# A decoder step on one core: the paged-cache stream ended earlier, and the second half's output projection moved in between two pairs of the first half's feed-forward slices

## The chip, the cores and the metric

The kernel runs on one core of a Trainium2 chip. Five engines take instructions from queues of their own, each in the order in which the program was built: PE (TensorE, matrix products; its weight loads are listed apart as PEld), DVE (VectorE), ACT (ScalarE), POOL (GpSimd) and SP (SyncE, which here only issues transfers). They wait for one another through semaphores. The metric is the time of one execution in microseconds (us) of device time; lower is better. Products accumulate in PSUM, everything else is held in SBUF, and large arrays lie in the memory outside.

## The reference

One layer of a hybrid decoder, for a prompt of 1024 tokens and for 8 sequences of 8 new tokens each that look back on 8192 cached positions. Cut to what matters:

```python
n = rmsnorm(h, g_mix);  u = n @ w_in                    # 1024 -> 2224 columns
o_gla = gated_linear_attention(u...)                    # 4 heads, chunked
q, ckv, krope = latents(u...)                           # MLA: 8 heads, latent width 128
o_mla = attend(q, ckv, krope)     # prompt: causal over 1024; sample: over 8192 cached positions
h = h + concat(o_gla, o_mla) @ w_o                      # output projection, 1024 x 1024
n = rmsnorm(h, g_ffn)
a, c = n @ ffn_w_gate, n @ ffn_w_up                     # 1024 -> 2816 each
h = h + (silu(causal_conv3(a)) * c) @ ffn_w_down        # 2816 -> 1024
h = h + (p @ ple_w_proj) * sigmoid(rmsnorm(h, g_ple) @ ple_w_gate)

def sample_attention(...):        # for each of 64 pages per sequence
    c, r = pool_ckv[page], pool_krope[page]             # gathered through the page table
    k, v = latent_to_kv(c, r)                           # keys are normalised per head
    stats = combine(stats, block_stats(q, k, v))        # running maximum, sum, weighted values
```

All products are made from float32 numbers that are split in two: a rounded high part and a low part, and three products (high x high, high x low, low x high) stand for one.

## The kernel before

There are two streams of work. The **cache stream** (`cache_stream`) attends the 8 sample sequences to their pages: 64 blocks of 1024 positions each. For a block, two indirect transfers on POOL's queue gather latents (`craw`) and rotary keys; PE transposes them (`ctp`, `crp`) and multiplies them with the key weights and the absorbed queries (`ks`: three products for each of two halves of each of eight row groups, so 48 a block and 3120 in all with the sequences' own new rows). ACT squares the keys (`csq`) and copies the scores (`sn`); DVE sums the squares (`css`); then ACT, DVE and POOL make the scale, the maximum (`mt`, with two small products on PE), the exponentials (`phl`), and PE multiplies with the latents (`cpv`, eight products). After the last block `po_mla` takes the result through the value weights and leaves it in `oTm`, which the output projection of the sample rows reads.

The **dense stream** (`dense`) does everything else, in this order: the input projections of the prompt's first and second half of 512 rows (`prompt_half`), gated linear attention, the prompt's causal attention, the first half's output projection (`wo_half(0)`), and the first half's 22 feed-forward slices of 128 columns (`ffn_half(0)`). Slices go in pairs: `ff_chunk` makes the gate and up products of a slice (`ps_gu`), and `down` multiplies a pair with its rows of the down weights (`ps_dn`) and adds them to the residual `h`. Behind the dense stream and not interleaved with the cache stream come the second half's output projection (`wo_half(1)`, which takes the 64 sample rows with it: `ps_ds`), the second half's feed-forward slices (`ffn_half(1)`), and the gated layer embedding.

How the two streams are mixed is set by a loop that emits a step of the cache stream whenever its due time is not past the work of the dense stream so far; each cache step moves the due time on by 4.4 times an entry of `PACE`, one entry for each part of the dense stream. What the loop emits goes to a scheduler that orders each engine's instructions by its own model of when they can run, with the emitted order as priority; so the order on the engines is fixed when the program is built, and is near the emitted one but not equal to it.

The second half's part needs space that the cache stream holds: three PSUM banks (`psK`) and a region of SBUF (`cp`). Both are given back at `ph1.close()`, after the loop, and then become `psT` (transposes and one more bank) and `xr`, which holds the second half's residual `h1`, the sample rows `hs`, the normalised and transposed input `X1`, and more. `wo_half` ends with the second normalisation: `renormer` takes a row tile's sum of squares on ACT (`junk`), the scale on POOL (`rs`), the scaled rows on DVE or on ACT and POOL (`xs`), transposes on PE in groups of four (`pt`), and a split by ACT and DVE into `X`. `ff_chunk` reads `X` whole.

## Time and profile before

| | |
|---|---|
| time, median of 3 runs | 2305.02 us (2301.93 to 2313.23) |
| the profiled execution: time / span | 2310.78 us / 2309.1 us |
| granted PE clock over the span | 0.985 |
| busy: PE, DVE, ACT, POOL | 2205.9, 1567.9, 1403.6, 1023.9 us |
| first and last score product of the cache stream (`ks`) start at | 68.1 and 1653.6 us |
| `po_mla` runs at | 1675.0 us |
| transfers over the span | mean 90 GB/s |

The span is divided here into the input projections (to about 400 us), gated linear attention (to about 600 us), the prompt's attention (to about 1005 us), the first half's output projection (to about 1100 us), its feed-forward slices with the cache stream beside them (to 1656 us), the end of the cache stream (to 1677 us), the second half's output projection (to 1730 us), its normalisation (to 1756 us), and the second half's feed-forward slices and the layer embedding. A view by windows gives for each stretch how long each engine was busy; PE's busy time subtracted from the length is time in which PE stood still. PE is counted as busy from the first to the modelled end of overlapping products, so two products of 512 columns that each last 0.39 us may start 0.23 us apart. The clock column is the share of full speed that PE was granted.

### The profile page before, as it was taken

How to read it: one execution, taken by the hardware profiler on the slowest of the kernel's cores; microseconds unless marked ns; L12 is line 12 of the kernel's file. 1: busy time of each engine (PE TensorE's matmuls, PEld its weight loads, DVE VectorE, ACT ScalarE, POOL GpSimd, SP SyncE). 2: the span in 40 equal slices, each digit the busy share in tenths (PEclk: the TensorE clock that was granted, in tenths of full speed). 3: DMA queues.
4: the chain of work that ended last, by engine and by line, in shares of the span. 5: the costliest groups of instructions: out<-in, count | busy, mean ns of one | idle time of the engine just before them, and what ended most of it. 6: DMA issues, size and time to landing. Idle time of an engine off the chain costs nothing.

```text
span 2309.1 us, 38976 instructions
## 1 busy us (share of the span) xinstructions
PE 2205.9 (96%) x13855; PEld 1952.7 (85%) x13855; DVE 1567.9 (68%) x2590; ACT 1403.6 (61%) x3758; POOL 1023.9 (44%) x1223
## 2 busy tenths in 40 slices
PE   7999999999999999999999999999798999999999
PEld 6889888788888888878788888878667999999999
DVE  5765684778878788878755666666677656666642
ACT  6666666768788888876655467767635323232431
POOL 6665675766867777664532234444313000000100
PEclk9999999999999999999999999999898999999999
DMA  5343343323322122143332232222142223232131
GB/s 185 110 133 112 102 152 124 100 69 96 95 75 64 58 58 60 40 143 110 90 93 85 85 100 79 78 78 67 39 138 74 85 81 91 75 92 74 52 116 39
DMA packets 228531, 207.67 MB, mean 90 GB/s; under 512 B 41326, under 2 KB 190291, under 8 KB 228339
## 3 DMA queue, kind: packets, MB, share of 16 engines
q1 hardware_dynamic: 216051, 163.23, 23.5%
q0 software_dynamic: 12288, 41.95, 5.8%
q8 instruction: 111, 1.82, 0.3%
q14 instruction: 81, 0.66, 0.1%
HBM read 178.56 MB, written 26.53 MB: 89 GB/s over the span
## 4 chain that ended last, share of the span: by engine, by line
PE 54%; ACT 5%; DVE 5%; DMA 4%; POOL 3%; issue 2%; POOLq 0%; SPq 0%; DVEq 0%; ACTq 0%
PE ps_gu L137 6%; PE ps_gu L138 6%; PE ps_gu L139 6%; PE ps_dn L137 4%; PE ps_dn L138 4%; PE ps_dn L139 4%; PE ks L137 3%; PE ks L139 2%; PE ks L138 2%; PE ps_pg L139 1%; PE ps_pg L137 1%; PE ps_pg L138 1%; PE cpv L605 1%; PE ctp L518 1%; DMA stg<-ffn_w_gate 1%
## 5 line engine op out<-in xcount | busy, mean ns | idle before, releaser
L542 ACT ACTIVATE csq<-ks 128x256 f32<-128x256 f32 x1040 | 389.2, 400 | 91.1 <-PE ks L139 85.1
L547 DVE TENSOR_REDUCE css<-csq 128x16 f32<-128x1024 f32 (+1 forms) x264 | 315.9, 1197 | 81.0 <-ACT csq L542 75.4
L138 PE MATMUL ps_gu<-X,guh 128*128 128x320 f32 (+2 forms) x1056 | 349.0, 331 | 0.0
L139 PE MATMUL ps_gu<-X,gul 128*128 128x320 f32 (+2 forms) x1056 | 348.4, 330 | 0.0
L137 PE MATMUL ps_gu<-X,guh 128*128 128x320 f32 (+2 forms) x1056 | 348.3, 331 | 0.1
L137 PE MATMUL ks<-mv0h,cTh 128*128 128x256 f32 (+1 forms) x780 | 249.2, 320 | 10.6 <-ACT sn L544 7.3
L138 PE MATMUL ks<-mv0l,cTh 128*128 128x256 f32 (+1 forms) x780 | 225.8, 291 | 0.0
L139 PE MATMUL ks<-mv0h,cTl 128*128 128x256 f32 (+1 forms) x780 | 222.4, 292 | 0.0
L139 PEld LDWEIGHTS ps_gu<-X,gul 128*128 128x128 f32 x1056 | 199.9, 189 | 14.4
L138 PEld LDWEIGHTS ps_gu<-X,guh 128*128 128x128 f32 x1056 | 199.7, 189 | 14.6
L137 PEld LDWEIGHTS ps_gu<-X,guh 128*128 128x128 f32 x1056 | 199.3, 189 | 15.0 <-ACT X L116 0.4
L116 ACT CAST guh<-stg 128x512 fp32r<-128x512 f32 x188 | 111.4, 620 | 149.2 <-PE ps_gu L138 70.4
L137 PE MATMUL ps_dn<-wdh,sh 128*128 128x512 f32 x480 | 188.4, 400 | 3.6 <-DVE h L1406 2.6
L138 PE MATMUL ps_dn<-wdl,sh 128*128 128x512 f32 x480 | 189.1, 394 | 0.0
L139 PE MATMUL ps_dn<-wdh,sl 128*128 128x512 f32 x480 | 179.7, 395 | 0.0
L1406 DVE TENSOR_TENSOR h<-h,ps_dn 128x512 f32<-128x512 f32 x240 | 154.4, 680 | 34.3 <-PE ps_dn L139 33.9
L137 PEld LDWEIGHTS ks<-mv0h,cTh 128*128 128x128 f32 x780 | 148.1, 190 | 33.2 <-ACT sn L544 16.6
L574 POOL TENSOR_TENSOR chl<-craw,chl 128x1024 fp32r<-128x1024 f32 x64 | 141.8, 2215 | 62.7 <-ACT chl L573 62.1
L117 DVE TENSOR_TENSOR gul<-stg,guh 128x512 fp32r<-128x512 f32 x138 | 94.5, 708 | 101.3 <-ACT guh L116 97.6
L138 PEld LDWEIGHTS ks<-mv0l,cTh 128*128 128x128 f32 x780 | 148.3, 190 | 7.8 <-issue 1.3
L593 POOL TENSOR_TENSOR phl<-sn,phl 128x512 fp32r<-128x512 f32 (+1 forms) x64 | 85.8, 1340 | 147.5 <-ACT phl L592 147.3
L139 PEld LDWEIGHTS ks<-mv0h,cTl 128*128 128x128 f32 x780 | 145.8, 189 | 1.2
(556 smaller groups left out, 6302.4 us busy)
## 6 DMA issues: line engine op xcount, KB each, us to landing
stg<-ffn_w_gate SPq DMA_DIRECT2D x88, 256.0 KB
stg<-ffn_w_up SPq DMA_DIRECT2D x88, 256.0 KB
stage<-ffn_w_down SPq DMA_DIRECT2D x88, 256.0 KB
stage<-w_in SPq DMA_DIRECT2D x48, 256.0 KB
stage<-w_o SPq DMA_DIRECT2D x32, 256.0 KB
h<-x_prompt SPq DMA_DIRECT2D x8, 512.0 KB
oraw<-doT SPq DMA_DIRECT2D x16, 256.0 KB
stg<-ple_w_gate SPq DMA_DIRECT2D x16, 256.0 KB
```

The lines of the kernel that those rows point to most:

```text
L116: act.copy(hi, src)
L117: (lo_eng or dve).tensor_tensor(lo, src, hi.bitcast(F32), ALU.subtract)
L137: pe.matmul(ps, ah, bh, start=first, stop=False)
L138: pe.matmul(ps, ah, bl, start=False, stop=False)
L139: pe.matmul(ps, al, bh, start=False, stop=last)
L518: pe.transpose(tp[:, i, :], craw[:, i, :], ident)
L542: act.activation(sq[:, f * 256:f * 256 + 256], ks[:, 0:256], AF.Square)
L547: dve.tensor_reduce(o.ss[:, g0 + i + 1 - n:g0 + i + 1, :].rearrange("p i h -> p (i h)"), sq2[:, :n].rearrange("p i (h n) -> p (i h) n", n= ...
L574: pool.tensor_tensor(ch[:, c0:c1, 128:256], src, ch[:, c0:c1, 0:128].bitcast(F32), ALU.subtract)
L593: pool.tensor_tensor(phl[:, :nt, 64:128], sb, phl[:, :nt, 0:64].bitcast(F32), ALU.subtract)
L605: pe.matmul(pv[:, 0:258], phl[:, i, :], o.ch[:, i, :], start=i == 0, stop=i == nt - 1)
L1406: dve.tensor_tensor(h, h, ps, ALU.add)
```

## The change

Four things are changed.

- The nine entries of `PACE` become smaller (the first from 2.0 to 1.41, the last from 1.34 to 1.1), so the loop emits cache steps at shorter intervals of dense work, and the stream is used up within the fourth pair of `ffn_half(0)`, as emitted.
- `dense` runs the first nine pairs of `ffn_half(0)` (slices 0 to 17), then asks for whatever is left of the cache stream (`z["drain"]`), then runs `wo_half(1)`, and then the last two pairs (slices 18 to 21). Their `down` takes its PSUM banks from the wider rotation `both`.
- The exchange of the cache stream's space for `psT` and `xr` becomes a function, `second_pools`, that is called when the cache stream has been emitted whole, in the middle of the first half's slices.
- `wo_half(1)` no longer ends with the last steps of its normalisation: these are called once right after it and after each of the two slices of the last pair. Its row tiles 4 to 7 are scaled in buffers of `xr` (`ptl`, `pth`). The first feed-forward weights of the second half are asked for before the last `down` of the first half.

```diff
-PACE = [2.0, 1.5, 2.2, 1.65, 1.6, 1.0, 1.45, 1.37, 1.34]
+PACE = [1.41, 1.088, 1.601, 1.168, 1.142, 0.708, 1.035, 1.1, 1.1]
+LASTG = 18
...
-        yield from ffn_half(0)
+        yield from ffn_half(0, range(0, LASTG, 2))
+        z["drain"] = True
+        yield 0.0
+        yield from wo_half(1)
+        z["step"](None)
+        for g in range(LASTG, NF, 2):
+            for f in (g, g + 1):
+                yield from ff_chunk(f, 0)
+                if g == NF - 2:
+                    z["step"](None)
+            if g == NF - 2:
+                ff_weights(0, 1)
+            yield from down((g, g + 1), both, 0)
...
-          (False, 4): "cca", (False, 5): "sca", (False, 6): "guh", (False, 7): "gul", (False, 8): "pth",
+          (False, 4): "ptl", (False, 5): "pth", (False, 6): "ptl", (False, 7): "pth", (False, 8): "pth",
...
-            step = renormer(False, p2t if hf else pd) if g == 3 else None
+            step = None
             if g == 3:
-                ff_weights(0, hf)
+                step = z["step"] = renormer(False, p2t if hf else pd)
                 if hf:
                     step(NT)
+                else:
+                    ff_weights(0, hf)
             yield from down(grp, bank, hf, step)
-        step(None)
-        step(None)
+        if not hf:
+            step(None)
+            step(None)
...
+    def second_pools():
+
+        ph1.close()
+        z["psT"] = ctx.enter_context(tc.tile_pool(name="psT", bufs=2, space=PSUM, reuse_waits="tile"))
+        xr = z["xr"] = ctx.enter_context(tc.tile_pool(name="xr", bufs=1, side="right", reuse_waits="tile"))
+        z["h"].append(xr.tile([P, 4, D], F32, name="h1"))
+        z["X"].append(xr.tile([P, 8, 2, 512 + R], F32R, name="X1"))
+        z["hs"] = xr.tile([R, D], F32, name="hs")
+        z["cout"] = xr.tile([P, 18, NF], F32, name="cout")
...
-        if live_c and (not live_d or due <= tdense):
+        if live_c and (not live_d or due <= tdense or "drain" in z):
             due += 4.4 * PACE[z["part"]]
             live_c = next(cs, done) is not done
             ncache += 1
+            if not live_c:
+                second_pools()
...
-    run(wo_half(1))
```

Three places show what the order becomes on the engines. First PE at the end of the cache stream. Before, the last score products stand among the products of the first half's eleventh pair, and these rows follow (`cpv`, `mt`, `pt_ol` and `po_mla` are the cache stream's last steps, `ps_dn` is the eleventh pair's, `ps_ds` the second half's output projection for the sample rows):

```order
L139 MATMUL ps_dn<-wdh,sl 128x512
L605 MATMUL cpv<-chl,phl 128x258 x8
L581 MATMUL mt<-ident,ml 128x128
L588 MATMUL mt<-ident,bm 128x64
L605 MATMUL cpv<-chl,phl 128x258 x8
L627 MATMUL pt_ol<-ident,acclo 128x64
L668 MATMUL po_mla<-oTm,WvT 64x64 x8
L1418 MATMUL ps_ds<-wdh,oTg 128x512
```

Now the last score products stand in the sixth pair, and `po_mla` stands among the gate and up products of the seventh:

```order
L139 MATMUL ps_gu<-X_14671,guh 128x512
L140 MATMUL ps_gu<-X_14671,gul 128x512
L669 MATMUL po_mla<-oTm,WvT 64x64 x8
L138 MATMUL ps_gu<-X_14671,guh 128x512
L139 MATMUL ps_gu<-X_14671,guh 128x512
```

What moved is the place of the stream's last steps: before, no dense product stood between them; now there are 49 products of 512 columns between the last score product's block and the first `mt`, 33 more up to the last `cpv`, and 54 from there to `po_mla`.

Second, PE at the end of the second half's output projection, where the normalised rows `xs` are transposed (`pt`). Before, the last products of the projection are followed by the transposes and then by the first gate products of the second half, whose operand `X` is what the transposes make:

```order
L139 MATMUL ps_dn<-wdh,sl 128x512
L1474 MATMUL pt<-ident,xs 128x64 x8
L1474 MATMUL pt<-ident,xs 128x128 x16
L137 MATMUL ps_gu<-X_21044,guh 128x256 x2
L1474 MATMUL pt<-ident,xs 128x128 x4
L138 MATMUL ps_gu<-X_21044,guh 128x256
```

Now the tenth pair of the first half follows the projection, and the transposes stand among its products (the sample rows' after 34 of them, the first prompt tile's, shown here, after 61):

```order
L138 MATMUL ps_gu<-X_14671,guh 128x512
L1487 MATMUL pt<-ident,xs 128x128 x4
L139 MATMUL ps_gu<-X_14671,guh 128x512
L1487 MATMUL pt<-ident,xs 128x128 x4
L140 MATMUL ps_gu<-X_14671,gul 128x512
```

What moved is the first reader of `X1`: it now comes two pairs after the projection, and what stands between reads the first half's `X`.

Third, ACT in the first half's input projections, where `G` takes four projected gate chunks out of PSUM. Before, these rows stand around the first two of them (`chl`, `cTh`, `kTh` and `csq` are the cache stream's; `w`, `st` and `gsf` the dense stream's):

```order
L161 COPY st<-ps_sm 64x256
L116 CAST w<-stage 128x4x128 x2
L689 COPY G<-ps_pj 128x512
L573 CAST chl<-craw 128x8x128
L689 COPY G<-ps_pj 128x512
L289 COPY gsf<-ps_sm 64x128
```

Now, from the first of them on:

```order
L690 COPY G<-ps_pj 128x512
L507 COPY sr<-csr 128x512
L557 ACTIVATE cy<-css,epst_68 128x64
L599 ACTIVATE mb<-bm 128x1
L558 ACTIVATE cy<-cy 128x64
L559 ACTIVATE ca<-cy 128x64
L543 ACTIVATE csq<-ks 128x256 x2
L545 COPY sn<-ks 128x64
L543 ACTIVATE csq<-ks 128x256
L117 CAST cTh<-ctp 128x512
```

More of the cache stream stands between two dense steps. Counted on PE, the score products that stand ahead of the second half's input projections are 309 before and 384 now; ahead of gated linear attention's first gate product 597 and 771; ahead of the first product of the first half's output projection 2244 and 2496; ahead of its first gate product 2412 and 2700. ACT's loads of a function table, which stand where the functions of the feed-forward slices and of the cache stream alternate, are 63 before and 43 now.

More of the change, by code (lines that the diff above doesn't have):

```diff
@@ L1514, in conv_state, with wo_half @@
         z["prv"] = prev.rearrange("p (b j f) -> p f b j", b=8, j=2)
-    def wo_half(hf):
+    def wo_half(hf, pairs=range(4)):
         bank = z["both"] if hf else pd
-        if hf:
-            sp.dma_start(z["hs"], A["x_sample"].rearrange("b t d -> (b t) d"))
-        for t in range(4 * hf, 4 * hf + 4):
-            sp.dma_start(hrows(t), A["x_prompt"][0, t * P:(t + 1) * P, :])
-        for g in range(4):
+        if pairs[0] == 0:
+            if hf:
+                sp.dma_start(z["hs"], A["x_sample"].rearrange("b t d -> (b t) d"))
+            for t in range(4 * hf, 4 * hf + 4):
+                sp.dma_start(hrows(t), A["x_prompt"][0, t * P:(t + 1) * P, :])
+        for g in pairs:
             grp = (2 * g, 2 * g + 1)
@@ L1612, in ff_chunk, with ffn_half @@
         chunks[f] = (sh, sl, ss_) + wdown(A["ffn_w_down"][0][fs, :])
-    def ffn_half(hf, hooks={}):
+    def ffn_half(hf, groups=range(0, NF, 2), hooks={}):
         bank = z["both"] if hf else pd
-        for g in range(0, NF, 2):
+        for g in groups:
             for f in (g, g + 1):
@@ L1622, in ffn_half, with p2t, p2, both @@
                 down_sample([chunks[c][2:] for c in (g, g + 1)], bank)
+    def p2t(shape, name):
+        return z["psT"].tile(shape, F32, tag="t", name=name)
+    def p2(shape, name):
+        return z["psT"].tile(shape, F32, tag="b", name=name, bufs=1)
+    turn = [0]
+    def both(shape, name):
+        turn[0] = (turn[0] + 1) % 6
+        return (pd, pm, pd, pm, pd, p2)[turn[0]](shape, name)
+    z["both"] = both
+    def second_pools():
[6 more added lines that the diff above has]
+        z["cout"] = xr.tile([P, 18, NF], F32, name="cout")
     dn = dense()
```

20 lines of the change are left out of this document (2 added, 18 removed).

## The prediction

> **What bounds the kernel now.** I read the page first. PE is busy nearly all the time and the other engines are not, so what can be won is time in which PE stands still or runs at a lower clock, and the slices show where that is: the 29th to the 31st, with 7, 9 and 8 in PE's row and 8, 9 and 8 in the clock's.
>
> ```profile
> span 2309.1 us, 38976 instructions
> PE 2205.9 (96%) x13855; PEld 1952.7 (85%) x13855; DVE 1567.9 (68%) x2590; ACT 1403.6 (61%) x3758; POOL 1023.9 (44%) x1223
> PE   7999999999999999999999999999798999999999
> PEclk9999999999999999999999999999898999999999
> ```
>
> Then the view by windows, cut at the stages (columns: length, busy time of PE, PEld, DVE, ACT and POOL, granted clock, transfers):
>
> ```profile
> core 0: us, PE busy (x) PEld busy (x) DVE busy (x) ACT busy (x) POOL busy (x), PEclk, DMA share, GB/s
> 140.00:250.00 110.00, 108.63 (x731) 100.55 (x730) 56.98 (x94) 67.45 (x200) 66.56 (x77) 1.00 0.39 125
> 250.00:400.00 150.00, 141.60 (x869) 125.86 (x868) 99.81 (x175) 99.99 (x293) 96.33 (x103) 0.99 0.41 129
> 600.00:1005.00 405.00, 391.54 (x2676) 341.54 (x2676) 326.40 (x542) 345.99 (x1027) 295.35 (x302) 1.00 0.22 63
> 1100.00:1350.00 250.00, 244.73 (x1195) 203.48 (x1195) 164.48 (x234) 137.23 (x296) 87.34 (x90) 0.99 0.31 92
> 1350.00:1656.00 306.00, 296.43 (x1617) 251.79 (x1617) 212.46 (x303) 224.23 (x534) 122.91 (x110) 0.99 0.24 74
> 1656.00:1677.00 21.00, 6.49 (x37) 5.22 (x35) 4.40 (x12) 5.08 (x10) 5.92 (x5) 0.58 0.16 52
> 1677.00:1730.00 53.00, 49.86 (x205) 37.91 (x205) 41.41 (x66) 20.08 (x39) 5.63 (x6) 0.97 0.39 126
> 1730.00:1756.00 26.00, 14.76 (x88) 12.84 (x88) 19.75 (x25) 19.74 (x51) 15.96 (x23) 0.74 0.17 52
> 1756.00:2200.00 444.00, 443.95 (x2926) 418.22 (x2927) 276.80 (x514) 154.44 (x309) 45.92 (x120) 1.00 0.27 81
> ```
>
> PE's idle time is the length less the busy time: 1.4 and 8.4 us in the two stretches of the input projections, 13.5 us in the attention, 5.3 and 9.6 us in the first half's slices, then 14.5 us of 21 at the cache stream's end and 11.2 us of 26 at the second normalisation. From 1756 us on there is nothing left to win. Two short stretches hold 25.7 us of idle time, and the waits of PE there say on what:
>
> ```profile
> PE mt L581 <- POOL ml L569: 7.9, 1, 7.9
> PE pt L1474 <- DVE X L117: 5.3, 3, 2.3
> PE pt L1474 <- POOL xs L1464: 4.4, 2, 3.8
> PE cpv L605 <- POOL phl L593: 3.5, 1, 3.5
> ```
>
> The first and the fourth are the last block of the cache stream going through ACT, POOL and DVE with no other product in the queue; the other two are the rows of the second half on their way to `X`.
>
> **The change, part by part.** *The cache stream's end.* Its chain, from the last score product (PE's timeline, then the chain of waits):
>
> ```profile
> 1653.19 0.30 PE L139 MATMUL ks<-mv1h,cTl 128*128 128x320 f32 x1
> 1653.33 0.28 PE L137 MATMUL ks<-mv0h,cTh 128*128 128x256 f32 x1
> 1653.45 0.28 PE L138 MATMUL ks<-mv0l,cTh 128*128 128x256 f32 x1
> 1653.57 0.27 PE L139 MATMUL ks<-mv0h,cTl 128*128 128x256 f32 x1
> ...
> 1655.10 0.40 PE L137 MATMUL ps_dn<-wdh,sh 128*128 128x512 f32 x1
> 1655.34 0.39 PE L138 MATMUL ps_dn<-wdl,sh 128*128 128x512 f32 x1
> ```
>
> ```profile
> 1664.80 0.49 PE mt L581
> ...
> 1669.96 2.10 PE cpv L605 x8
> ...
> 1675.03 1.97 PE po_mla L668 x16
> ```
>
> Products of 512 columns start about 0.23 us apart (1655.10 to 1655.34). The last score product starts at 1653.57; `mt` is 11.2 us behind it, `cpv` 16.4, `po_mla` 21.5. In the new order 49, 82 and 136 products of the sixth and seventh pair stand ahead of these three, which is 11.3, 18.9 and 31.3 us of cover. The chain gets ACT, DVE and POOL no longer alone, and `mt` has nothing to spare, so I leave 1 us (bounds 0, where the cover suffices, and the old 14.5): -14.5 + 1.
>
> *The second normalisation.* It now has the tenth and eleventh pair beside it. The old starts of the transposes, on PE's timeline:
>
> ```profile
> 1731.33 0.46 PE L1474 MATMUL pt<-ident,xs 64*128 64x64 f32 x4 [1.39 <-DVE xs L1461]
> ...
> 1736.25 1.11 PE L1474 MATMUL pt<-ident,xs 128*128 128x128 f32 x4 [3.79 <-POOL xs L1464]
> ```
>
> PE had done the projection 1.39 us before 1731.33; the sample rows come at that time and the first prompt tile 6.3 us after it. The new order puts 34 and 61 products ahead of them, 7.8 and 14.0 us. But DVE must now scale two row tiles ahead of the multiplication that frees a PSUM bank of the tenth pair, so some waiting will return: I take 3 us, between 0 and the old 11.2, nearer to the covered end: -11.2 + 3. The projection's own 3.1 us of idle time stay: its weights pass the same three staging buffers. The new buffers for the scaled rows are first used again in the second half's slices, where PE has no idle time; moving the pools issues no instruction. Both at nothing.
>
> *The clock.* In both stretches PE is granted about half speed (length, PE busy, clock, transfers):
>
> ```profile
> 1660.00:1670.00 10.00, 1.20 (x4) 0.50 0.00 0
> 1670.00:1680.00 10.00, 7.37 (x32) 0.51 0.65 233
> 1730.00:1740.00 10.00, 3.15 (x16) 0.72 0.29 84
> 1740.00:1750.00 10.00, 7.48 (x38) 0.60 0.16 52
> ```
>
> Busy time times the missing share is 0.6 + 3.6 + 0.9 + 3.0 = 8.1 us. Where PE has products throughout, the rows around show 1.00, so this goes with the idle time: -8.1.
>
> *The first half's slices.* They hold 708 score products before (3120 less 2412) and 420 now (less 2700), in the same dense manner while they last, about 100 a pair: 9.6 us of idle time (1350 to 1656 us) for about 520 of them (by the order, from the seventh pair on) gives 7.2 for the some 390 that the order has behind the first pair, and the thinner pairs' idle time, 1.2 us behind the start, falls away: -3.6 (bounds 0 and -6). ACT also loses table loads, 63 before and 43 now. One and what follows it, in the chain of waits:
>
> ```profile
> 1654.55 1.28 ACT L556
> 1655.85 0.35 ACT cy L556
> ```
>
> The next function starts 0.02 us after the load, so 20 x 1.28 = 25.6 us of ACT go. I count them at nothing, since PE's idle time there already holds what of them PE felt. [...]
>
> *The denser stages.* 174 more score products (771 less 597), 3.6 blocks of 48, run before linear attention, and 78 more between there and the output projection. The work is moved, not added; only more idle time costs. At 0.12 to 0.14 us from one score product to the next (1653.19 to 1653.45) 174 are 23 us, so 140 to 400 us becomes about 290 us with the stream's other products. There is room in the first part:
>
> ```profile
> 160.00:180.00 20.00, 20.00 (x107) 16.97 (x106) 2.42 (x7) 6.95 (x17) 9.68 (x8) 1.00 0.39 111
> 320.00:340.00 20.00, 18.15 (x132) 17.06 (x131) 18.89 (x32) 13.25 (x44) 15.99 (x17) 1.00 0.49 157
> ```
>
> DVE and ACT are idle most of the first slice; in the second DVE is busy 94% of the time and PE idle 9%. If all became like 250 to 400 us (5.6% idle): 290 x 0.056 = 16.2 against 9.8 now, +6.5. If all became like the slice at 320: 26.8, +17. If PE filled its holes with the moved work: down to -3. The first is the nearest row, the same work a little denser: +6.5. The attention, with ACT busy 85% and PE idle 3.3%, gets its part of the 78, on 1647 before (2244 less 597), so some 5% more of the stream: 0, at worst 5% idle, +7.
>
> *The sum:* -13.5 - 8.2 - 8.1 - 3.6 + 6.5 = -26.9 us on the profiled execution's 2310.8 (its span 2309.1 and 1.7 around it), so 2283.9. The median of the runs is 5.8 lower, 2305.0; the same difference gives 2278.1, and I say 2278.
>
> **The rivals.** *SP held up.* The loads of `hs` and `h1` need the cache stream's space, and SP waits for it with the feed-forward weights behind. Before, that wait was 20.1 us, and the four transfers followed it:
>
> ```profile
> SPq L1520 <- PE cpv L605: 20.1, 1, 20.1
> ...
> 1672.70 2.00 SPq L1522 DMA_DIRECT2D h<-x_prompt  x4
> ```
>
> 2.25 MB at the 233 GB/s of the window at 1670 are 9.7 us more, 30 us in all. Now they stand between the two down loads of the eighth pair's first slice. The weights behind them are first needed after the seventh pair's second slice, its `down` and the eighth's first slice: about 144 products, 33 us. So it decides from 33 us on. As SP comes there when `po_mla` is due a microsecond or two later, I expect about 12 us, hidden; if SP came a full wait early and the loads were slow, up to 20 us would be seen: 2298.
>
> *The denser stages eat the gain.* At the worst rows above, +17 and +7 in place of +6.5, and no gain in the slices: 2278 + 17.5 + 3.6 = 2299. For it: DVE's 94% at 320 us. Against it: the two slower engines are busy 52 to 67% over 140 to 400 us.
>
> *Slower.* Place: the input projections. The 3.6 moved blocks could run there as the last block does at 1656, each with its chain exposed: 14.5 us of idle time a block, 52 us, 2278 - 6.5 + 52 = 2323.5. It outweighs the 33.4 us of the other terms from 64% exposure on. Against it: the present stream runs there at 1.3 to 5.6% of idle time, with dense products between its steps, and only ahead of the queue's end was nothing there to fill.
>
> *PE's busy time hides room.* Weight loads (PEld) cover 81% of 1100 to 1350 us and 94% from 1756 us on:
>
> ```profile
> L138 PEld LDWEIGHTS ps_gu<-X,guh 128*128 128x128 f32 x1056 | 199.7, 189 | 14.6
> ```
>
> If the loads set the pace, the five pairs that now run without the stream (5 x 144 x 0.23 = 166 us) could be up to 13% faster: 21 us, 2257. Against it: a load of 0.19 us in the 0.23 to 0.24 us from one product of 512 columns to the next is 79 to 83% already, so these pairs stand at their pace. [...]
>
> *The change does not do what it says.* In the order the stream ends in the sixth pair, not the fourth, but three pairs still stand between it and the moved projection, and it can't slip further: the order is fixed. It is part of the forecast.
>
> **How the numbers follow.** About 0.5% (11.5 us) is what a measurement of this kernel can tell from no change. Forecast, 2268 to 2293: 0.62. More is won (PE's holes filled, the slices at their best), about 2262: 0.07. Hidden room, 2257: 0.03. SP held up, 2285 to 2298, half of it within 0.5%: 0.08. Denser stages eat the gain, about 2299: 0.12. Slower, about 2324: 0.08. So faster 0.62 + 0.07 + 0.03 + 0.04 = 0.76, same 0.12 + 0.04 = 0.16, slower 0.08. The range 2258 to 2300 leaves out the slower case, half of the denser one and the lowest, some 0.17 in all.
>
> **What would show it.** Right: in the new profile `po_mla` lies far ahead of the second half's `ps_ds` with PE busy around both; the waits of `mt` for `ml` and of `pt` for `xs` are gone or under 2 us each; the clock is 1.00 from the cache stream's end to the layer embedding; idle time up to 400 us grows by less than 10 us. Wrong: idle time before 1000 us that grows by more than 25 us, with `ks` or `crp` waiting for ACT and DVE; a hole in the eighth pair with `guh` or `wdh` late; or a half clock at the two new borders.

## The result, and the profile after

| | before | after |
|---|---|---|
| time, median of 20 runs each | 2308.58 us (2301.93 to 2315.36) | 2313.19 us (2307.01 to 2320.55) |
| ratio after to before, 95% interval | | 1.0018 (1.0009 to 1.0027) |
| span of the profiled execution | 2309.1 us | 2310.9 us |

The change does not pay: 0.2% slower, inside the 0.5% that count as no change. The forecast was 2278 us, and its range ended at 2300. The page of the kernel after (the busy times and the two rows of slices):

```profile
span 2310.9 us, 38951 instructions
PE 2213.8 (96%) x13855; PEld 1952.6 (84%) x13855; DVE 1574.1 (68%) x2590; ACT 1379.8 (60%) x3738; POOL 1027.6 (44%) x1223
PE   7989998999999999999999999899999999999999
PEclk9989999999999999999999999999999999999999
```

The hole of the 29th to 31st slice is gone, and so is its lower clock. In its place there are 8s in PE's third, seventh and 26th slice, the third with a lower clock as well, and PE is busy 7.9 us longer with the same 13855 products.

The new place does what was wanted. From the view by tile of `ps_ds` and from PE's timeline after (the number in brackets is the idle time ahead of the instruction):

```profile
L1431 PE MATMUL ps_ds<-wdh,oTg x8: 389/395/499, 1617.8 to 1637.3; 128*128 128x512 f32 x8
```

```profile
1499.15 0.79 PE L138 MATMUL ps_dn<-wdh,sh 128*128 128x512 f32 x1 [4.10 <-DVE cv L1620]
1502.91 0.27 PE L582 MATMUL mt<-ident,ml 128*128 128x128 f32 x1
1511.16 1.12 PE L606 MATMUL cpv<-chl,phl 128*128 128x258 f32 x8
1525.25 1.15 PE L669 MATMUL po_mla<-oTm,WvT 128*64 128x64 f32 x16
```

`po_mla` (1525.25) stands 92 us ahead of the first sample product (1617.8), and `mt` and `cpv` start without any idle time ahead of them. The view by windows after, from ahead of the stream's end to the second normalisation's end, and the second half's slices:

```profile
1450.00:1500.00 50.00, 43.92 (x222) 36.07 (x221) 33.72 (x44) 33.21 (x69) 19.85 (x17) 0.99 0.20 58
1500.00:1527.00 27.00, 27.00 (x126) 21.31 (x126) 16.70 (x32) 12.18 (x21) 4.88 (x6) 0.95 0.28 81
1700.00:1752.00 52.00, 48.52 (x211) 38.44 (x210) 29.27 (x43) 19.14 (x38) 11.83 (x16) 0.97 0.28 86
1752.00:2177.00 425.00, 425.00 (x2769) 399.17 (x2768) 266.99 (x497) 144.74 (x292) 48.83 (x120) 1.00 0.28 82
```

The stream's end (1500 to 1527) has no idle time at all, where it had 14.5 us; its clock is 0.95, behind the wait of 4.10 us just ahead of it. What was won here, and 1.8 us more by the spans, must have been lost elsewhere. The same view, cut at the same places of the program in both kernels (columns as in the prediction: length, busy time of PE, PEld, DVE, ACT, POOL, granted clock, transfers): the four parts of the input projections, linear attention, and the first half's slices to the second normalisation's end. Before:

```profile
0.00:144.50 144.50, 124.04 (x695) 109.70 (x696) 97.93 (x199) 94.98 (x293) 91.15 (x138) 0.94 0.45 139
144.50:230.20 85.70, 85.15 (x594) 78.53 (x592) 42.44 (x72) 52.03 (x145) 47.68 (x46) 1.00 0.40 130
230.20:328.20 98.00, 92.71 (x529) 81.81 (x530) 70.44 (x139) 68.88 (x225) 69.52 (x92) 1.00 0.38 117
328.20:407.10 78.90, 74.40 (x498) 68.35 (x496) 45.26 (x59) 48.43 (x131) 50.42 (x53) 0.98 0.46 139
407.10:602.80 195.70, 189.66 (x1426) 164.45 (x1427) 151.47 (x256) 148.06 (x488) 142.61 (x199) 1.00 0.31 90
...
1119.40:1744.00 624.60, 587.16 (x2978) 488.52 (x2978) 417.42 (x601) 382.18 (x863) 218.19 (x213) 0.97 0.28 84
```

And after:

```profile
0.00:149.90 149.90, 125.28 (x693) 111.55 (x694) 101.32 (x202) 96.16 (x294) 92.20 (x139) 0.91 0.44 134
149.90:253.40 103.50, 102.25 (x719) 94.53 (x718) 60.99 (x93) 69.88 (x204) 65.80 (x67) 1.00 0.36 115
253.40:375.20 121.80, 111.84 (x656) 100.49 (x654) 93.92 (x168) 87.37 (x290) 82.59 (x98) 0.97 0.35 109
375.20:452.90 77.70, 74.11 (x505) 68.16 (x503) 33.75 (x53) 50.21 (x131) 50.15 (x57) 1.00 0.49 142
452.90:668.20 215.30, 208.37 (x1496) 177.28 (x1497) 161.98 (x274) 158.90 (x514) 145.03 (x202) 0.98 0.29 82
...
1202.80:1751.80 549.00, 527.29 (x2555) 430.40 (x2554) 359.45 (x523) 294.98 (x640) 170.17 (x169) 0.99 0.30 91
```

The stages hold different numbers of score products now, so their lengths can't be compared as they stand. To compare them I give every product its own time: the usual interval from one product of its shape to the next in the profile of before (0.118 us for a score product of 256 columns, 0.146 for one of 320, 0.231 for 512 columns; the value that 40% of the intervals stay under). All products together have 2083.2 us in every kernel of this case. This is an estimate: with the usual interval taken a little differently the losses of single stages shift by up to 6 us, in all kernels alike, and the changes between kernels by less than 1.5 us. What a stage takes beyond its products' own time is its loss, whether PE is seen idle, runs at half clock, or is held up for so short that the records still show it busy. The 225.9 us of loss before and the 227.7 after divide like this (us):

| stage | loss before | after | change | of it idle | at half clock | inside PE's busy time |
|---|---|---|---|---|---|---|
| input projections | 60.6 | 74.6 | +14.0 | +8.6 | +5.2 | +0.1 |
| linear attention | 20.2 | 31.7 | +11.5 | +0.9 | +3.3 | +7.3 |
| attention, first half's output projection | 70.3 | 73.7 | +3.4 | +2.0 | -1.8 | +3.2 |
| first half's slices, second half's output projection and normalisation | 63.5 | 40.6 | -22.9 | -15.7 | -4.9 | -2.2 |
| from there to the end | 11.3 | 7.2 | -4.1 | | | |

27 us are won at the new place, and 29 are lost ahead of it, by the order that was made denser to let the stream end early.

### The profile page after: what moved, and what is told of

It is laid out like the page before. It is cut to its first block, busy times and chain, and to the rows that moved or that the text cites. A ratio compares the mean times of both kernels' runs of the same rounds, so it can differ in the third digit from the quotient of the medians.

```text
span 2310.9 us, 38951 instructions
## 1 busy us (share of the span) xinstructions
PE 2213.8 (96%) x13855; PEld 1952.6 (84%) x13855; DVE 1574.1 (68%) x2590; ACT 1379.8 (60%) x3738; POOL 1027.6 (44%) x1223
## 4 chain that ended last, share of the span: by engine, by line
PE 72%; DVE 10%; ACT 8%; DMA 4%; POOL 3%; issue 3%; SPq 0%; DVEq 0%; ACTq 0%; POOLq 0%
PE ps_gu L138 6%; PE ps_gu L139 6%; PE ps_gu L140 6%; PE ks L138 4%; PE ps_dn L138 4%; PE ks L140 4%; PE ps_dn L139 4%; PE ks L139 4%; PE ps_dn L140 4%; PE cpv L606 2%; PE ctp L519 2%; PE ps_lt L279 2%; DVE css L548 1%; PE ps_pj L138 1%; PE ps_pg L140 1%
## 5 line engine op out<-in xcount | busy, mean ns | idle before, releaser
L1419 DVE TENSOR_TENSOR h<-h,ps_dn 128x512 f32<-128x512 f32 x240 | 154.3, 680 | 40.6 <-PE ps_dn L140 40.2
L118 POOL TENSOR_TENSOR gul<-stg,guh 128x512 fp32r<-128x512 f32 x50 | 68.7, 1394 | 183.7 <-ACT guh L117 183.5
```

The source lines that it names most:

```text
L118: (lo_eng or dve).tensor_tensor(lo, src, hi.bitcast(F32), ALU.subtract)
L1419: dve.tensor_tensor(h, h, ps, ALU.add)
```

## The experiments

In all of them "the late place" is the changed kernel's place of the second half's output projection. Every kernel of a group ran beside the kernel before; the edits are to `PACE` unless a diff shows more. `PACE` is not the order itself: the scheduler makes the order from it, so I give the number of score products that the order has ahead of linear attention (597 before, 771 after). The first theory was that the denser order ahead of the slices costs what the new place wins; its rival, that the stream's work costs PE the same wherever it stands, and the new place itself brings little.

**The two parts of the change, each alone.** The kernel before with the new numbers:

```
-PACE = [2.0, 1.5, 2.2, 1.65, 1.6, 1.0, 1.45, 1.37, 1.34]
+PACE = [1.41, 1.088, 1.601, 1.168, 1.142, 0.708, 1.035, 1.1, 1.1]
```

> The new table of paces in the kernel before, with the second half's output projection left behind the first half's slices. The order on every engine is the changed kernel's up to the second pair's slices, so the early stages are the same work in the same order. Theory A (the denser early order itself costs what the new place wins): up to the first gate product of the slices it takes the changed kernel's 1202.8 us, not the 1119.4 of before, of which some 29 us are not work; the cache stream's end is covered (-14.5 idle and some -4 of clock), the second normalisation is not, so about 2315, 2308 to 2322. Theory B (the early loss of that one profile is chance, the denser order is as good as the other): the end's 18 us are won, about 2290.

Measured: 2322.22 us, ratio 1.0052 (1.0038 to 1.0067), at the upper end of theory A's range and far from theory B's 2290. The denser order alone is a loss. Up to the slices it loses what the changed kernel loses (75.3 us in the input projections, 31.9 in linear attention), and the slices with the second normalisation lose 49.1. The move of the output projection is the difference to the changed kernel: 9 us by the medians, 13 by the losses of the stages from the slices on (60.9 against 47.8; the profiled execution of this version is its slowest, 2326.34 us).

The changed kernel with the old numbers:

```
-PACE = [1.41, 1.088, 1.601, 1.168, 1.142, 0.708, 1.035, 1.1, 1.1]
+PACE = [2.0, 1.5, 2.2, 1.65, 1.6, 1.0, 1.45, 1.37, 1.34]
```

> The changed kernel with the old table of paces: the early stages are in the order of the kernel before, and what is left of the cache stream at the ninth pair (213 score products in PE's order) is run out ahead of and beside the second half's output projection. Theory A: no early loss, the second normalisation covered (-11.2 idle, -4 clock), the stream's end beside the output projection's products only in part: 2290 to 2300. Theory B (cache work costs the same idle time wherever it is put): the 213 products run with too little beside them, 2300 to 2312.

Measured: 2317.28 us, ratio 1.0034 (1.0024 to 1.0044), slower than both theories had it. Here 213 score products are still left when the output projection's place is reached, and they run there with little beside them: the input projections and linear attention lose 60.8 and 20.5 us as before, the slices' stage 74.8 instead of 63.5. With this order the move costs more than it wins: it does not pay by itself, only where the stream has ended ahead of it.

**The same place, with the density taken later.** The old order up to linear attention's end and a denser one from the attention on (the changed kernel's move kept):

```
-PACE = [1.41, 1.088, 1.601, 1.168, 1.142, 0.708, 1.035, 1.1, 1.1]
+PACE = [2.0, 1.5, 2.2, 1.65, 1.6, 1.0, 0.9, 0.8, 0.7]
```

> The changed kernel with the old paces up to linear attention and smaller ones behind it (0.9, 0.8, 0.7): the order is the one of before up to the first half's output projection and second pair; then some 100 score products a pair, the stream ending in the eighth pair, so its end and the normalisation are covered as in the changed kernel. Theory A: the new place wins its 27 us and no early stage gets denser: 2280 to 2288. Theory B (cache work costs the same wherever it is put, and the slices now hold all 708 of it in eight pairs): the slices give back most of it, 2300 to 2310.

The old order up to linear attention, the new numbers from there on (the last one smaller, 0.9):

```
-PACE = [1.41, 1.088, 1.601, 1.168, 1.142, 0.708, 1.035, 1.1, 1.1]
+PACE = [2.0, 1.5, 2.2, 1.65, 1.142, 0.708, 1.035, 1.1, 0.9]
```

> The changed kernel with the old paces for the input projections of both halves only; denser from linear attention on, as in the changed kernel, and a little more in the slices (0.9). 549 score products stand in linear attention's stage as in the changed kernel (525 before). Theory A by density, stage by stage: the input projections take the time of before (14 us of the loss gone), linear attention still loses its 11.5 us (215 us against 196): 2288 to 2296. If linear attention's loss came from the order alone and not from the stream's density, the stage takes about 200 us and the whole 2280 to 2286.

Measured: 2293.55 us, ratio 0.9929 (0.9916 to 0.9942), and 2291.36 us, ratio 0.9928 (0.9913 to 0.9943). Both are faster than either kernel by 15 us and more. The input projections lose 61.6 and 60.5 us again, as before the change. Of the 22.9 us won in the slices' stage the first, which leaves 708 score products to that stage, keeps about 10, and its total is above theory A's 2280 to 2288; the second, with 615 left, keeps all. In the second, linear attention takes 207.2 us for 549 score products, where the changed kernel takes 215.3 for as many: by the same count it loses about 5 us more than before the change, not 11.5. So the first theory holds: the place was right, and the early order was the loss. Its rival is right in so far as the slices too lose more when more of the stream is left to them.

**Where in the early order?** The new numbers for the input projections, the old ones for linear attention:

```
-PACE = [1.41, 1.088, 1.601, 1.168, 1.142, 0.708, 1.035, 1.1, 1.1]
+PACE = [1.41, 1.088, 1.601, 1.168, 1.6, 1.0, 1.035, 1.1, 1.1]
```

> The new PACE for the input projections (771 score products ahead of linear attention, as in the changed kernel), the old one for linear attention, the rest of the stream in the attention and the output projection; the new place of the output projection. By the theory that each stage loses by its own density, the input projections lose their 14 us again and linear attention its 11 to 12 us no longer: time beyond the products' own from the start to linear attention about 75 us, in linear attention 20 to 22 us, total 2299 to 2305 us. By the rival that linear attention loses by what stands ahead of it (a chain that comes late into it), it stays at 29 to 32 us there and the total is 2308 to 2314.

Measured: 2312.19 us, ratio 1.0009 (0.9998 to 1.0020), no better than the changed kernel. The input projections lose 73.6 us, as expected, but linear attention keeps its 30.7. This alone does not refute the theory that each stage loses by its own density, because linear attention got 549 score products here too, although its own numbers are the old ones. What speaks against it stands beside it: with 549 products linear attention loses 30.7 us here and some 25 to 26 in the version above, and the kernel before loses 20.2 with 525.

Half-way between the old numbers and the new in the input projections (669 score products):

```
-PACE = [1.41, 1.088, 1.601, 1.168, 1.142, 0.708, 1.035, 1.1, 1.1]
+PACE = [1.705, 1.294, 1.9, 1.409, 1.6, 1.0, 1.035, 1.1, 1.1]
```

> A PACE half-way between old and new in the input projections (669 score products ahead of linear attention, against 597 and 771), the old one in linear attention; the new place of the output projection. If the loss grows in proportion to the products moved, the time beyond the products' own from the start to linear attention is 66 to 69 us (60.6 before, 74.7 with the new PACE) and the total 2294 to 2298. If there is room up to a point and a steep loss behind it, it stays at 60 to 62 and the total is 2288 to 2292. If any shift of the order costs the whole, 73 to 76 and 2299 to 2304.

Measured: 2286.44 us, ratio 0.9891 (0.9867 to 0.9916), faster than all three theories had it. Its input projections lose 59.0 us, less than before, with 72 products more in them, and linear attention 21.9. So 72 more products cost the input projections nothing, and 174 cost them 14 us. That is not a price per product. Two theories remain: a limit of rate between the two, or single steps that come late in some orders and in others not.

The profiles first point to the second. PE's timeline after, shortly ahead of the first gated values, and DVE's and POOL's at the same time:

```profile
127.24 0.28 PE L140 MATMUL ks<-mv0h,cTl 128*128 128x256 f32 x1
132.76 0.58 PE L140 MATMUL csr<-qbd0h,kTl 128*128 128x256 f32 x1 [5.24 <-DVE kTl L118]
...
139.59 0.60 PE L519 MATMUL ctp<-ident,craw 128*128 128x128 f32 x4
144.97 0.69 PE L589 MATMUL mt<-ident,bm 64*128 64x64 f32 x2 [4.78 <-DVE mt L588]
```

```profile
125.49 2.07 DVE L104 SCALAR_TENSOR_TENSOR qrs<-nwt,qrs 128x16 f32<-128x16 f32 x1
127.49 1.21 DVE L548 TENSOR_REDUCE css<-csq 128x16 f32<-128x1024 f32 x1
128.62 3.09 DVE L328 TENSOR_TENSOR qt<-qt,qrs 128x512 f32<-128x512 f32 x1
131.63 0.41 DVE L331 TENSOR_TENSOR qt<-qt,qrs 128x256 f32<-128x256 f32 x1
131.97 0.41 DVE L894 TENSOR_REDUCE kss<-sqk 128x4 f32<-128x256 f32 x1
132.29 0.41 DVE L118 TENSOR_TENSOR kTl<-crp,kTh 128x256 fp32r<-128x256 f32 x1
```

```profile
126.22 1.31 POOL L565 TENSOR_TENSOR sn<-sn,sr 128x512 f32<-128x512 f32 x1
...
128.66 2.49 POOL L118 TENSOR_TENSOR w<-stage,w 128x512 fp32r<-128x512 f32 x2
```

PE's next product needs `kTl`, a step of 0.41 us on DVE. In this order it stands behind the dense stream's own work on DVE: a normalisation (`qrs`, `qt`) in which one step takes much longer than in the half-way order, 3.09 us for `qt` 128x512 against 0.68, while POOL works at the same time. In the timeline no later product of PE starts ahead of the waiting one, and PE stands for 5.2 us. At the same place, in the half-way order, `kTl` has less ahead of it, though one such step of DVE took 3.05 us there as well:

```profile
133.37 0.38 PE L140 MATMUL csr<-qbd0h,kTl 128*128 128x256 f32 x1 [1.96 <-DVE kTl L118]
```

```profile
129.33 0.68 DVE L328 TENSOR_TENSOR qt<-qt,qrs 128x512 f32<-128x512 f32 x1
129.93 3.05 DVE L331 TENSOR_TENSOR qt<-qt,qrs 128x256 f32<-128x256 f32 x1
132.90 0.41 DVE L118 TENSOR_TENSOR kTl<-crp,kTh 128x256 fp32r<-128x256 f32 x1
```

The second wait of the dense order, 4.78 us for `mt`, is not in the half-way order at all. The clock is 0.50 behind each of the two long waits, and 1.00 behind the half-way order's 1.96 us. Windows after (the wait for `kTl`, behind it, the wait for `mt`, behind it), and the half-way order's wait for `kTl` and what follows:

```profile
129.50:133.00 3.50, 0.24 (x1) 0.24 (x2) 3.50 (x5) 0.59 (x2) 2.86 (x3) 0.64 0.75 234
133.00:137.00 4.00, 4.00 (x18) 4.00 (x19) 3.45 (x5) 2.99 (x11) 2.53 (x5) 0.50 0.30 81
...
139.50:144.10 4.60, 0.69 (x7) 0.45 (x5) 4.21 (x7) 1.54 (x7) 3.59 (x3) 1.00 0.01 2
144.10:147.50 3.40, 2.42 (x8) 1.96 (x8) 3.26 (x9) 1.21 (x3) 1.80 (x2) 0.50 0.60 182
```

```profile
131.00:133.40 2.40, 0.44 (x5) 0.24 (x3) 2.40 (x3) 0.49 (x2) 2.40 (x3) 1.00 0.70 218
133.40:137.00 3.60, 3.60 (x26) 3.33 (x27) 3.46 (x8) 3.07 (x11) 3.60 (x4) 1.00 0.22 64
```

The next two runs tell the theories apart. The half-way order up to the gated values, the new numbers behind them (747 products):

```
-PACE = [1.41, 1.088, 1.601, 1.168, 1.142, 0.708, 1.035, 1.1, 1.1]
+PACE = [1.705, 1.088, 1.601, 1.168, 1.6, 1.0, 1.035, 1.1, 1.1]
```

> The half-way order up to the first gated values (PE's instructions are the same up to its 635th row), the new PACE for the rest of the input projections (747 score products ahead of linear attention), the old one in linear attention. In the profiles so far the dense order has two waits of PE for DVE ahead of the gated values, 5.2 and 4.8 us, where the half-way order has one of 2.0. If the loss lies in single late steps, these two are gone here: 35 to 37 us beyond the products' own up to the gated values (41.4 and 35.9 in the dense and the half-way order), the rest of the input projections keeps its 30 to 33, and the total is 2298 to 2306. If it goes by the number of products moved, the sum up to linear attention is 70 to 73 and the total 2304 to 2310.

Three quarters of the way (720 products), which shares PE's first 672 rows with the dense order (the new numbers in the input projections):

```
-PACE = [1.41, 1.088, 1.601, 1.168, 1.142, 0.708, 1.035, 1.1, 1.1]
+PACE = [1.56, 1.19, 1.75, 1.29, 1.6, 1.0, 1.035, 1.1, 1.1]
```

> 720 score products ahead of linear attention (597 before, 669 half-way, 771 dense), the old PACE in linear attention; PE's first 672 rows are those of the dense order, with its two waits for DVE. If the loss lies in single late steps, it keeps the 41 us beyond the products' own up to the gated values and may be anything from 24 to 32 behind them: 65 to 73 up to linear attention, total 2295 to 2305. If there is a limit of rate between 669 and 771 products, it is a third to a half of the way: 64 to 67, and 2292 to 2298.

Measured: 2300.78 us, ratio 0.9958 (0.9944 to 0.9972), and 2302.27 us, ratio 0.9958 (0.9944 to 0.9973). The losses of the input projections in two parts, up to the first gated values and behind them, and of linear attention (us):

| order | score products ahead of linear attention | up to the gated values | behind them | linear attention |
|---|---|---|---|---|
| before | 597 | 36.7 | 23.9 | 20.2 |
| half-way | 669 | 35.9 | 23.1 | 21.9 |
| three quarters | 720 | 42.1 | 29.9 | 34.9 |
| first part half-way | 747 | 35.1 | 38.7 | 27.2 |
| dense (the new numbers in the input projections alone) | 771 | 41.4 | 32.2 | 30.7 |
| after | 771 | 42.4 | 32.3 | 31.7 |

Where PE's first rows are those of the half-way order, the two waits and their 6 us are gone; where they are those of the dense order, they are there, whatever the number behind. But the first-part order, with 24 products fewer than the dense one, loses 6.5 us more behind the gated values, over the 30 to 33 expected, and three quarters loses most in linear attention with the fewest products there of these orders (504 against 510 and 549; the kernel before has 525 and loses 20.2). The longest waits there are other ones each time. The views of waits (us in total, times, longest), of the first-part order ahead of the second half's gated values and of three quarters in linear attention:

```profile
PE ps_kv L138 <- ACT qt L321: 4.5, 1, 4.5
PE crp L497 <- ACT pvs L609: 2.2, 1, 2.2
PE ps_pj L138 <- ACT w L117: 2.1, 1, 2.1
```

```profile
PE pa L1130 <- POOL kx L1121: 4.9, 1, 4.9
PE crp L497 <- DVE pvs L611: 2.6, 1, 2.6
```

Both totals lie where the theory of single late steps had them, and three quarters lies outside the limit of rate's (64 to 67 us of loss, 2292 to 2298). The loss up to linear attention of the first-part order, 73.9 us, fits neither (65 to 70 by late steps, 70 to 73 by the number moved). So the runs favour single late steps, on ACT, DVE or POOL, which belong to an order and come back wherever that order stands in a kernel, as the two waits of 5.2 and 4.8 us do. They do not show it: no run takes one such step alone out of an order, and of the 11.5 us that linear attention lost in the changed kernel 7.3 lie inside PE's busy time, spread over many short hold-ups that no view of waits names. That all orders from 720 products on have some, and those up to 669 have few, says that the density makes them likelier; why the border lies between these two isn't settled. The total of the input projections alone (72.1, 73.9, 73.6 and 74.6 us from 720 products on) would also fit a step at a limit of rate; what speaks against it is that the places of the loss change and that fewer products can lose more.

**Lighter ACT and DVE steps.** If PE waits for ACT and DVE, shorter steps should bring the two orders together. Half the columns of the keys' sums of squares are left out, in the changed kernel and in the version with the density taken later:

```
-act.activation(sq[:, f * 256:f * 256 + 256], ks[:, 0:256], AF.Square)
+act.activation(sq[:, f * 256:f * 256 + 256].rearrange("p (h n) -> p h n", n=64)[:, :, 0:32],
+               ks[:, 0:256].rearrange("p (h n) -> p h n", n=64)[:, :, 0:32], AF.Square)
...
-                  sq2[:, :n].rearrange("p i (h n) -> p (i h) n", n=64), AX.X, ALU.add)
+                  sq2[:, :n].rearrange("p i (h n) -> p (i h) n", n=64)[:, :, 0:32], AX.X, ALU.add)
```

> The changed kernel, with half of the columns of each head left out of the sums of squares of the cache stream's keys: ACT squares 32 columns of each head's 64 and DVE sums as many, with the same number of instructions on every engine and the same products on PE, in the same order. To be compared with its partner, which leaves out the same and has the late order. If the denser early order loses its time because PE's next product waits for ACT's and DVE's steps of the stream, the 19.6 us between the two orders shrink to 5 to 12 us when these steps are shorter. If the loss is PE's own or comes from POOL, the transfers or the clock, they stay at 17 to 22 us.

> The same left out, in the version with the old PACE up to linear attention's end and the denser one from the attention on (2293.55 us with all columns). By the theory of waits for ACT and DVE it gains less than its partner in the changed kernel's order does, which comes to within 5 to 12 us of it; by the rivals both gain alike and stay 17 to 22 us apart.

Measured: 2292.53 us, ratio 0.9930 (0.9903 to 0.9957), and 2274.64 us, ratio 0.9841 (0.9821 to 0.9862). Both gain 19 to 21 us, and 17.9 stay between them instead of 19.6: the gap did not close, which is what the rivals had. But the runs don't decide: the scheduler answered the shorter steps with another order in both (in the traces PE's order is the old one for the first 331 products, to about 78 us, and not to the end as was expected; the lighter changed kernel has 729 score products ahead of linear attention instead of 771), so they compare two new orders. By stages the input projections are now 5.1 us apart (63.4 and 58.3) and linear attention 6.6 (26.3 and 19.7), where it was 13.0 and 11.3; the profiled executions are 12.0 us apart in all. Whether ACT's and DVE's length is what PE waits for stays open.

**Thinner early, and the best version.** Fewer products early than before (525) and more later:

```
-PACE = [1.41, 1.088, 1.601, 1.168, 1.142, 0.708, 1.035, 1.1, 1.1]
+PACE = [2.3, 1.72, 2.5, 1.9, 1.142, 0.708, 0.9, 0.8, 0.7]
```

> A thinner order than before in the input projections (525 score products ahead of linear attention, against 597 before and 669 half-way), the new PACE in linear attention, denser from the attention on. If less density early still gains, 54 to 58 us beyond the products' own up to linear attention (60.6 before) and a total of 2282 to 2288; if the early part has nothing left to gain, 59 to 62 and 2288 to 2294, as the two versions with the old early order.

Measured: 2307.68 us, ratio 0.9991 (0.9978 to 1.0005), slower than either theory allowed. The input projections lose 60.2 us, nothing less than before; linear attention 25.8 and the slices' stage 54.6 us. That stage loses 53 to 55 us in the two complete versions that leave 700 or more score products to it and still end the stream ahead of the moved projection, and 37 to 38 in those that leave 604 or 615.

The half-way order, denser from the attention on:

```
-PACE = [1.41, 1.088, 1.601, 1.168, 1.142, 0.708, 1.035, 1.1, 1.1]
+PACE = [1.705, 1.294, 1.9, 1.409, 1.7, 1.0, 0.95, 0.9, 0.8]
```

> The half-way order up to linear attention's end, and from the attention on a denser one (PACE 0.95, 0.9, 0.8 in the last three parts), so that the cache stream ends a pair earlier; the new place of the output projection. If what the stream loses in the attention and the slices goes by single late steps, the total is anywhere within 4 us of the half-way order's 2286; by the rate, 2 to 5 us above it.

Measured: 2284.16 us, ratio 0.9887 (0.9871 to 0.9904), the fastest of the complete kernels here, though not separable from the half-way order's 2286.44. Its losses are 58.1 us in the input projections, 20.4 in linear attention, 78.0 in the attention and the output projection, and 36.8 in the slices' stage. With its numbers the change is worth 1.1%. It too has a late step left: just behind linear attention's end PE waits 7.2 us for `maskq`, a step of POOL, and 10.2 us at half clock follow. The half-way order has the same wait (6.4 us), which the kernel before has not, and its attention and output projection lose some 84 us against 70.3; its profile is of the slowest of its four runs (2295.28 us).

## Why the prediction was wrong

- **The denser stages: this step failed.** It put +6.5 us for the whole, with 17 as the worst for the input projections and 7 for the attention. Measured: +14.0 in the input projections, +11.5 in linear attention, +3.4 in the attention and the output projection, 28.9 in all. It failed in three ways. It counted idle time only: of that the input projections got 8.6 us more, close to the 6.5, but the half clock behind the waits brought 5.2 us on top. It put linear attention at nothing without a reason; the loss there lies mostly inside PE's busy time (7.3 of 11.5 us), where a row of idle time can't show it. And it took a mean share of idle time from the neighbouring stretch of the old order, which does not hold the new order's own late steps, such as the two waits of 5.2 and 4.8 us, of which the old one has only the first, at 2.0 us. That the denser order costs what the move wins is shown by the runs that change one of the two alone; by which mechanism it costs, late steps or a limit of rate, is in part argued.
- **The rival that came nearest** was that the denser stages eat the gain, at 2299 us. It had nothing for linear attention either, and idle time alone as its cause, so that its sum came so near is in part luck. Its price was too low by about 5 us (28.9 against 24), the gain fell 3 us short of the 29.8 that it left, and the median of before over 20 runs is 3.6 us above the one from which it was reckoned. The rival "slower", with each moved block's chain exposed, was not what happened: the blocks ran with dense products between, and PE waited at a few steps.
- **The stream's end** came out: no idle time from 1500 to 1527 us against 14.5 at its old place, and the wait of `mt` for `ml` is gone. What is late next is a wait of 4.1 us for `cv` just ahead, at 1499 us.
- **The second normalisation** came out: the long waits of `pt` for `xs` are gone, and 1.2 us is the longest for `X` in the changed kernel. Beside the denser order without the move, the move is worth 9 to 13 us; the prediction had 8.2 for this step and some 4 for its clock.
- **The clock** came out at the two borders, but for one stretch at each: 0.95 from 1500 to 1527 us and 0.97 from 1700 to 1752 us are 3.4 us each at half speed, behind waits of 4.1 and 2.1 us. That stages without idle gaps keep their clock was right (1.00 from 1752 to 2177 us, with PE busy throughout); that new waits elsewhere would pay the same price was not thought of.
- **The first half's slices** were to win 3.6 us. In total the stages from the slices on win 27.0 us where the four terms gave 33.4: what is missing stands as new waits in this stage, in the view of waits after (for `h` it was 1.9 us in two waits before):

```profile
PE ps_dn L138 <- DVE h L1419: 6.5, 8, 2.1
PE ps_dn L138 <- DVE cv L1620: 5.0, 3, 4.1
```

- **SP held up** did not come: in SP's timeline after, the loads of `hs` and `h1` go out as soon as `po_mla` has run, the weights' loads go on at 1532.6 us, and PE has no wait over 1.1 us from there to 1640 us:

```profile
1526.12 0.34 SPq L156 DMA_DIRECT2D stage<-ffn_w_down  x1
1526.50 0.51 SPq L1534 DMA_DIRECT2D hs<-x_sample  x1
1527.06 2.92 SPq L1536 DMA_DIRECT2D h<-x_prompt  x4
1532.64 0.33 SPq L156 DMA_DIRECT2D stage<-ffn_w_down  x1
```

- **PE's busy time hides room:** not at the products of 512 columns, where the pairs without the stream keep their 0.231 us. But PE's busy time did hide a loss: it grew by 7.9 us with the same products. A score product is recorded as 0.28 us and the next started after 0.12 (1653.33 to 1653.45 us before), so a hold-up of up to 0.16 us behind each still counts as busy.
- **The signs named beforehand** were badly chosen. Idle time grew by 8.6 us in the input projections, under the 10 that were to show the forecast right, and by 10.8 up to the attention's end, under the 25 that were to show it wrong; and still the kernel lost 27 us there.

## What to carry to other kernels

Moving work into an earlier stage costs what the new order loses there, and a mean share of idle time from a neighbouring stage of the old order does not price that. Count a stage's loss against its products' own time, since idle time missed the half clock behind the waits (here 5.2 us in the input projections) and the short hold-ups inside PE's busy time (7.3 us in linear attention). Where a table of numbers sets an order, try the move and the density apart and at two or three doses: here the same move went with 0.2% lost in one order, and with 1.1% won in another.

## What the runs showed of the hardware

- **A wait can cost more than its length.** In the fourteen profiles of this case (start and end left out) every low-clock stretch is at 0.50, and all but two of the 148 last 3.4, 6.8, 10.2 or 13.7 us (one of the two, at 1659 us before, lasts 20.5). In the traces before and after, products of 512 columns start 0.427 us apart in such stretches and 0.231 otherwise. PE had idled for 0.9 to 4 us in the 4 us ahead of each stretch. Of PE's waits from 0.5 to under 1 us 59 in 378 have such a stretch beside them or within 4 us behind, of those of 1.5 to 2 us 32 in 73, of those from 2 us on 97 in 113, and of those from 3 us on 32 in 34. So the waits of 3 us or more were nearly all followed by at least 3.4 us at half clock. Where PE works throughout, that cost some 1.6 us more, an estimate from the two intervals (3.4 - 3.4 x 0.231 / 0.427). The wait of 1.96 us in the half-way order above had no such stretch behind it (1.00 from 133.4 to 137 us).
- **Some DVE steps beside POOL took several times as long.** `qt`, 128 x 512, took 0.68 us in one order and 3.09 in the other, and 128 x 256 took 0.41 and 3.05, each slow time with POOL at operations on two arrays of its own. In the fourteen profiles 31 of the 224 such steps took over 1 us, all with such an operation of POOL beside them; but so had 134 of the 191 that took under 0.8 us, so company alone does not decide it. No run here took POOL's work away to test what does.
